# Splitting the first load of a DMA-bound rotation kernel into 16 and 112 partitions

## The chip, the cores and the metric

The kernel runs on one core of one Trainium2 chip. The metric is the device time of one execution in microseconds (us); lower is better. All runs are with a granted TensorE clock of 1.0 (TensorE does nothing here).

## The reference

```
x: float32 of shape (32, 3, 256, 256)
return np.rot90(x, k=-1, axes=(-2, -1)).astype(np.float32)
```

Each of 96 images of 256 x 256 is turned by 90 degrees. Nothing is computed: 25.17 MB are read from HBM, rearranged on the chip, and 25.17 MB are written back.

## The kernel before

The work is cut into 12 slabs of 2 MB. All loads are issued first, from the SyncE queue, then VectorE transposes slab after slab in place of the slab before, and each finished slab is stored by the same queue. Slab 0 is turned first into PSUM and stored last.

```python
P, RI, RO, I = 128, 16, 8, 2          # F = RO * W = 2048 elements, 8 KB
ld8_v  = rows_in.rearrange("(n i p r) w -> n p i (r w)", i=I, p=P, r=RO)
ld16_v = rows_in.rearrange("(n i m r) w -> n i m (r w)", i=I, m=Q * K, r=RI)   # Q * K = 64
# ... units[n]: one SBUF tile of [P, I, F] for each slab, all resident

for n in range(n_slabs):
    if n == last:
        nc.sync.dma_start(out=units[n], in_=ld8_v[n])            # 2 MB
        continue
    for i in range(I):
        if n == 0:
            nc.sync.dma_start(out=units[n][:, i], in_=ld8_v[n][:, i])   # 1 MB, 128 rows of 8 KB
        else:                                                    # 1 MB, 64 rows of 16 KB, every 2nd partition
            nc.sync.dma_start(out=units[n][i::I].rearrange("p i f -> p (i f)"), in_=ld16_v[n, i])

# ... for each slab: two VectorE transposes, then stores from SyncE; slab 0 last
```

## Time and profile before

| | before |
|---|---|
| time, median of 6 runs | 124.09 us (123.96 to 124.23) |
| span of the profiled run | 122.2 us |
| packets on the 16 DMA engines, share of the span | 97.8% |
| VectorE busy | 76% |
| first packet starts | 1.74 us |
| full rate from about | 2.75 us |
| last store lands | 121.18 us |

The DMA engines move a transfer in packets, here one for each row (in the trace of the kernel before 3456 of 8 KB and 1280 of 16 KB), and an engine's part of a transfer has landed when it reports to the semaphore (16 reports for each of that trace's 37 transfers). A stretch line gives start:end, length, busy time of VectorE, ScalarE and GpSimd, the granted clock, the share of the DMA engines' time filled by packets, and the bytes of packets in GB/s. A packet counts in full in the stretch in which it starts, so a short stretch can show more than the true rate, and a share above 1. "The stream is late by d at so many MB" below means: the same count of bytes had been moved d us later than in the kernel before. It is worked out from all packets in the two traces, with the bytes of a packet spread evenly over its time; two further executions of the unchanged start, the control and the kernel with the last load in two, come out 0.07 and 0.08 us late at 10 MB, so a difference of 0.1 us is about the least that counts.

### The profile page before, as it was taken

What the parts mean: (1) busy time and instruction counts of PE and PEld (TensorE: products, weight loads), DVE (VectorE), ACT (ScalarE), POOL (GpSimd) and SP (SyncE); (2) the same over time, 40 slices, a digit from 0 to 9 for tenths busy, and PEclk for the clock granted to TensorE, in tenths of its full rate; (3) what the DMA queues carried; (4) which work ended last, traced back from release to release, by engine and by line L of the source; (5) the groups of instructions that cost most, each with busy time, mean ns of one, the idle gap of its engine ahead of it and who ended that gap; (6) DMA issues with size and microseconds to landing.
All of it is one profiled execution on the core that took longest, in us unless ns stands there. A gap on an engine that the chain in (4) does not pass through costs nothing.

```text
span 122.2 us, 134 instructions
## 1 busy us (share of the span) xinstructions
DVE 93.3 (76%) x24; ACT 5.0 (4%) x3; POOL 0.2 (0%) x4
## 2 busy tenths in 40 slices
DVE  0299999999999999999999999999999940000000
ACT  0000000000000000000040000000000651000000
POOL 0000000000000000000000000000000000000000
DMA  3999999999999999999999999999999999999993
GB/s 88 429 432 434 440 440 429 429 429 429 429 429 429 429 429 424 434 424 408 370 414 428 426 429 429 429 429 429 429 429 429 424 429 429 429 429 426 429 429 166
DMA packets 5584, 50.33 MB, mean 412 GB/s; under 512 B 592, under 2 KB 720, under 8 KB 848
## 3 DMA queue, kind: packets, MB, share of 16 engines
q1 hardware_dynamic: 5584, 50.33, 97.8%
HBM read 25.17 MB, written 25.17 MB: 412 GB/s over the span
## 4 chain that ended last, share of the span: by engine, by line
DMA 57%; DVE 13%; issue 7%; DVEq 3%; ACT 2%; SPq 1%
DMA u<-in_x_dram 39%; DMA out_dram<-u 18%; DVE u L82 10%; DVE u L76 3%; DVEq L119 3%; ACT u L92 2%; SPq L66 1%; SPq L89 0%
## 5 line engine op out<-in xcount | busy, mean ns | idle before, releaser
L82 DVE STREAM_TRANSPOSE u<-u 128x2048 f32<-128x2048 f32 x20 | 78.0, 3948 | 0.3
L76 DVE STREAM_TRANSPOSE turned<-u 128x2048 f32<-128x2048 f32 x2 | 7.6, 3828 | 5.5 <-DMA u<-in_x_dram 5.5
L76 DVE STREAM_TRANSPOSE u<-u 128x2048 f32<-128x2048 f32 x2 | 7.8, 3953 | 0.0
L92 ACT COPY u<-turned 128x2048 f32<-128x2048 f32 x2 | 3.7, 1866 | 33.8 <-DVE u L76 33.8
L92 ACT ACT_TABLE_LOAD x1 | 1.3, 1283 | 62.4 <-DMA u<-in_x_dram 62.4
L108 POOL MEMSET const-bfloat16-1.0<- 128x1 bf16 x1 | 0.1, 102 | 0.0
L108 POOL MEMSET const-uint8-127<- 128x1 uint8 x1 | 0.1, 102 | 0.0
L108 POOL MEMSET const-float32-0.0<- 128x1 f32 x1 | 0.1, 99 | 0.2 <-issue 0.2
L108 POOL MEMSET const-float32-1.0<- 128x1 f32 x1 | 0.1, 99 | 0.0
## 6 DMA issues: line engine op xcount, KB each, us to landing
u<-in_x_dram SPq DMA_DIRECT2D x22, 1024.0 KB, 19.6
out_dram<-u SPq DMA_DIRECT2D x11, 2048.0 KB, 25.0
u<-in_x_dram SPq DMA_DIRECT2D x1, 2048.0 KB, 22.5
out_dram<-u SPq DMA_DIRECT2D x1, 1024.0 KB, 20.2
out_dram<-u SPq DMA_DIRECT2D x1, 896.0 KB, 20.2
out_dram<-u SPq DMA_DIRECT2D x1, 128.0 KB, 20.6
```

The costliest lines, as they stand in the source:

```text
L66: nc.sync.dma_start(out=units[n][:, i], in_=ld8_v[n][:, i])
L76: nc.vector.transpose(out=dst[:, :, ::-1, ::-1], in_=src)
L82: nc.vector.transpose(out=dst[:, cs], in_=src[:, cs])
L92: nc.scalar.copy(out=units[last][:, i], in_=turned0[:, i])
L108: nc = _bacc.Bacc("TRN2", target_bir_lowering=False, num_devices=1)
L119: with _tile.TileContext(nc) as tc:
```

## The change

In the trace of the kernel before, the first 1 MB transfer is 128 packets of 8 KB and reports 16 landings, so eight rows for each of the 16 DMA engines if they are dealt out evenly. They do not start together: eight first packets start from 1.738 to 1.826 us, eight more only from 2.405 to 2.530. The idea of the change is that a first transfer with a single row for each engine gets all 16 engines going at once.

```diff
+    FIRST = 16
...
             if n == 0:
-                nc.sync.dma_start(out=units[n][:, i], in_=ld8_v[n][:, i])
+                for a, b in ((0, FIRST), (FIRST, P)) if i == 0 else ((0, P),):
+                    nc.sync.dma_start(out=units[n][a:b, i], in_=ld8_v[n][a:b, i])
```

## The prediction

> **What bounds the kernel now.** I read the page first, for who is busy; then the pieces of the chain that ended last, for what sets the end; then a table of stretches, for the transfer rate in the middle and at the two ends; and last the records of single packets in the first three microseconds, because the change sits there. The page:
>
> ```profile
> span 122.2 us, 134 instructions
> DVE 93.3 (76%) x24; ACT 5.0 (4%) x3; POOL 0.2 (0%) x4
> ...
> DMA  3999999999999999999999999999999999999993
> GB/s 88 429 432 434 440 440 429 429 429 429 429 429 429 429 429 424 434 424 408 370 414 428 426 429 429 429 429 429 429 429 429 424 429 429 429 429 426 429 429 166
> ...
> q1 hardware_dynamic: 5584, 50.33, 97.8%
> ```
>
> See that the 16 DMA engines are full in every slice but the first and the last, near 429 GB/s, and that their packets fill 97.8% of the span, while VectorE has 24% to spare. The 25.17 MB in and 25.17 MB out are fixed by the problem. 50.33 MB at 429 GB/s is 117.3 us; the span is 122.2, so moving things about can win at most 4.9 us. The chain, in order of time (start, length, what):
>
> ```profile
> 0.67 0.06 issue
> 0.73 0.39 SPq L66
> 1.12 0.05 issue
> 1.17 0.42 SPq L66
> 1.59 0.05 issue
> 1.64 8.74 DMA u<-in_x_dram
> ...
> 99.26 1.87 ACT u L92
> ```
>
> See that one issue of the first slab takes 0.39 us and the next starts 0.44 us after it. The last scalar copy ends at 101.13 us, and its store lands 20 us later: it queues behind stores already issued, so neither VectorE nor the copy is on the path at the end. The stretches (start:end, length, engines' busy time, clock, share of the DMA engines, GB/s):
>
> ```profile
> 1.50:1.75 0.25, 0.00 (x0) 0.00 (x0) 0.00 (x0) 1.00 0.08 33
> 1.75:2.00 0.25, 0.00 (x0) 0.00 (x0) 0.00 (x0) 1.00 1.62 229
> 2.00:2.25 0.25, 0.00 (x0) 0.00 (x0) 0.00 (x0) 1.00 0.53 66
> 2.25:2.50 0.25, 0.00 (x0) 0.00 (x0) 0.00 (x0) 1.00 0.57 197
> 2.50:2.75 0.25, 0.00 (x0) 0.00 (x0) 0.00 (x0) 1.00 0.27 98
> 2.75:3.00 0.25, 0.00 (x0) 0.00 (x0) 0.00 (x0) 1.00 1.00 426
> ...
> 100.00:120.00 20.00, 0.00 (x0) 1.12 (x1) 0.00 (x0) 1.00 1.01 428
> 120.00:120.50 0.50, 0.00 (x0) 0.00 (x0) 0.00 (x0) 1.00 0.55 229
> 120.50:121.20 0.70, 0.00 (x0) 0.00 (x0) 0.00 (x0) 1.00 0.06 23
> ```
>
> See that the engines start at about 1.74 us but do not run at full rate before about 2.75; from then to the end the stream has no hole. In the packet records, eight first packets of 8 KB start between 1.738 and 1.826, and six of these take 0.89 to 1.15 us where a steady one takes 0.309. The other two take 0.32, and their successors stall for 1.05 us. A second group of eight starts only between 2.405 and 2.530. By about 2.8 us every engine has done one packet, give or take 0.2. So the time is: start of the stream, plus 50.33 MB at a fixed rate, plus a tail of 1.0 us after the last landing at 121.18. The time of 124.06 is 1.9 us over the span, which I carry along unchanged.
>
> [...] The trace of before shows 16 landings for every transfer, of 128 or 64 rows. [...] the second eight engines start 0.667 us after the first eight, which for the 64 rows of half a transfer is 10.4 ns a row. [...] Here the first packet comes 1.01 us after the issue begins and 0.62 after it ends, so no early start before the end of the issue is seen. [...] The trace before has no load confined to 16 partitions, [...] its 64-row loads use every second partition, [...] and run at full rate.
>
> **The change, part by part.** No byte, VectorE or ScalarE instruction changes. The order of instructions shows one more transfer on the SyncE queue, a first transpose that waits for two semaphores instead of one, and the eight rotating transfer semaphores shifted by one.
>
> - Issue: one more of about 0.39 + 0.05 = 0.44 us on the SyncE queue. Later loads are issued 0.44 us later. Each 1 MB of load takes 2.45 us to move and about 0.64 to issue, so this is hidden from the third transfer on. Cost on the path: 0, except for the second.
> - What it is meant to win: with one row for each engine, [...]. The most that a perfect start could win is read from the stretches: up to 3.00 us the bytes are 0.25 x (33 + 229 + 66 + 197 + 98 + 426) = 262 KB; at 428 GB/s from 1.74 they would be 539 KB. The difference, 277 KB, is 0.65 us.
> - What takes it back: the 16 packets are done after 0.31 us, at about 2.1 to 2.2. The 112-row transfer is issued at 1.17 instead of 0.73, so its first packets come at 1.17 + 1.01 = 2.18, and by the same 10.4 ns a row the second eight get theirs 56 x 10.4 = 0.58 us later, at 2.76. These engines have then done one packet, as they have by 2.8 before. With this sum the eight late engines win some 0.05 to 0.1 us, not 0.6, and the end is set by the slowest engine.
> - [...]
> - Later in the kernel: the shift of the semaphores keeps every store waiting on the same load as before, since both moved by one. VectorE starts about 0.1 to 0.4 us earlier or later; its slack at the end is 20 us. Cost 0.
>
> The sum is a small gain of about 0.1 [...], half believed, [...]: about 0.05 us off, 124.0.
>
> **The rivals.**
> - The start is won in full: all 16 engines move from 1.8 us on and the second transfer arrives in time. For it: two first packets of before took only 0.32 us, so data can flow that early. Against: their next packets stalled for 1.05. It would give 124.06 - 0.65 = 123.4.
> - A cold start that lasts until about 2.45 us whatever is asked for, visible as the stall of early and late engines alike up to about 2.75. Then nothing is won; for it speaks that early and late starters finish together. 124.06.
> - The second issue is the new wait: if the stall repeats for the second transfer, [...], engines idle for up to 0.44 us. 124.5.
> - [...]
>
> **Range and chances.** Every mechanism acts once, in the first 3 us, and is bounded by 0.65 us of gain [...]. Two per cent is 2.5 us, which none reaches. The runs of before differ by 0.27 us. I predict 124.0, with 123.5 to 124.6 holding it 8 times in 10, chances of 0.01 faster, 0.98 same and 0.01 slower.
>
> **What would show it.** In the changed kernel's stretches, rates between 1.75 and 2.25 well above 229 and 66 with a hole after them mean that the first packets went early and the second issue came late; a full rate from 1.8 on means the first rival; [...]. Everything from 10 us on should be the same profile, shifted by the same amount. I would be wrong if that shift differed between start and end, if the rate in the middle changed, or if the time left 123.4 to 125.2.

The sum came to 124.0, which is 124.06 less 0.05, half of the gain of 0.1. Against the gain stood a loss of about 0.3 us, weighed at less than half, and with it a rival at 125.2 (the upper end of the last range named): estimates, on grounds that no trace or run shows. The estimate: the second eight engines would start 8 x 10.4 ns = 0.08 us after the first instead of 0.67, the 10.4 ns a row being the 0.667 us in the trace of the kernel before over 64 rows. That 16 rows are one for each engine was assumed; the trace of the changed kernel shows 16 first packets between 1.754 and 1.928 us.

## The result, and the profile after

The changed kernel took 124.58 us (median of 6 runs, 124.45 to 124.70) against 124.09 before. The ratio is 1.0037, with a 95% interval of 1.0025 to 1.0050: a loss of 0.4%, small but clear of noise. A ratio here is the mean time of one kernel's runs over that of the other's of the same rounds, so it is not quite the ratio of the medians.

The page after:

```profile
span 122.8 us, 136 instructions
...
GB/s 80 304 448 427 432 427 432 432 432 427 427 427 427 427 427 427 427 427 387 424 418 425 427 427 427 430 427 427 430 427 430 430 427 430 427 427 427 430 430 205
...
u<-in_x_dram SPq DMA_DIRECT2D x1, 896.0 KB, 5.6
...
u<-in_x_dram SPq DMA_DIRECT2D x1, 128.0 KB, 3.1
```

The rate in the middle is the same. The second slice, 3.1 to 6.1 us, shows 304 GB/s where before had 429: the loss sits there. The stretches of the changed kernel:

```profile
1.75:2.00 0.25, 0.00 (x0) 0.00 (x0) 0.00 (x0) 1.00 2.33 524
2.00:2.25 0.25, 0.00 (x0) 0.00 (x0) 0.00 (x0) 1.00 0.00 0
2.25:2.50 0.25, 0.00 (x0) 0.00 (x0) 0.00 (x0) 1.00 0.43 66
2.50:2.75 0.25, 0.00 (x0) 0.00 (x0) 0.00 (x0) 1.00 0.56 131
2.75:3.00 0.25, 0.00 (x0) 0.00 (x0) 0.00 (x0) 1.00 0.56 131
...
4.00:5.00 1.00, 0.00 (x0) 0.00 (x0) 0.00 (x0) 1.00 1.02 328
5.00:6.00 1.00, 0.00 (x0) 0.00 (x0) 0.00 (x0) 1.00 1.10 320
...
60.00:62.00 2.00, 1.97 (x2) 0.00 (x0) 0.00 (x0) 1.00 1.00 418
```

And two of the same stretches in the kernel before:

```profile
4.00:5.00 1.00, 0.00 (x0) 0.00 (x0) 0.00 (x0) 1.00 1.01 426
...
60.00:62.00 2.00, 1.97 (x2) 0.00 (x0) 0.00 (x0) 1.00 0.93 334
```

Three things are to be seen.

1. The early start happens. All 16 first packets begin between 1.754 and 1.928 us. They take 0.57 to 0.60 us each, so the 0 GB/s from 2.00 to 2.25 is no idle time: by the packets' durations the engines are all busy there. The gap follows when the first packets end (2.33 to 2.52 us), as the second ones straggle in from 2.343 to 3.1: from 2.50 to 2.75 the engines are busy for 28% of the time, from 2.75 to 3.00 for 52%. Up to 10 us they idle for 0.40 us each, against 0.30 before, and by 3.0 us 176 KB have been moved, against 210 KB before and 186 KB in the control. So the start is neither won nor lost by much.
2. From 3 to 6.5 us the engines are full (share 1.01 to 1.10 in the whole stretches), yet only 311 to 328 GB/s move. A packet of 8 KB takes 0.43 us (median of those that start from 4 to 6 us) instead of 0.309. Each packet counted with its excess over 0.309, this comes to 0.94 us for each engine between 3.0 and 6.5 us. The stream is 1.23 us late at 12 MB.
3. At 60 to 62 us the roles change: before has a slow spell of 334 GB/s at the end of the load phase, after has none. Of the 1.24 us late at 24 MB, 0.87 remain at 27 MB. At the end the last engine finishes 0.69 us late (121.87 against 121.18), as the engines end closer together (within 0.29 instead of 0.62 us), and the span is 0.6 longer.

So the change costs 1.2 us where it acts, and more than half of that does not show in the time.

### The profile page after: what moved, and what is told of

The parts are those of the page before. It is cut to its first block, busy times and chain, and to the rows that moved or that the text cites. A ratio compares the mean times of both kernels' runs of the same rounds, so it can differ in the third digit from the quotient of the medians.

```text
span 122.8 us, 136 instructions
## 1 busy us (share of the span) xinstructions
DVE 93.3 (76%) x24; ACT 5.0 (4%) x3; POOL 0.2 (0%) x4
## 4 chain that ended last, share of the span: by engine, by line
DMA 52%; DVE 16%; issue 10%; DVEq 3%; ACT 2%; SPq 0%
DMA u<-in_x_dram 36%; DMA out_dram<-u 16%; DVE u L84 13%; DVE u L78 3%; DVEq L121 3%; ACT u L94 2%; SPq L68 0%; SPq L88 0%
```

## The experiments

Theory P: which partitions a transfer writes sets its rate. The rival, theory L: the second transfer is issued too late, and the engines run dry. A third question is what gives 0.37 us back near 60 us (the expectations say 0.35). Every kernel gave a correct result, and all but the control differ from the kernel before (or from the changed one) only by the lines shown. Ratios are to runs of the kernel before on the same chip in the same rounds, whose medians were 123.95 to 124.01.

### Halves: the same sizes on other partitions

```diff
 # halves_contiguous
-nc.sync.dma_start(out=units[n][:, i], in_=ld8_v[n][:, i])
+for rows in (slice(0, 64), slice(64, P)) if i == 0 else (slice(0, P),):
+    nc.sync.dma_start(out=units[n][rows, i], in_=ld8_v[n][rows, i])
 # halves_interleaved: (slice(0, P, 2), slice(1, P, 2))
```

> The first 1 MB load as two transfers of 64 neighbouring partitions (0 to 63, then 64 to 127). Theory P ([...] the changed kernel's loss comes from which partitions one transfer writes; [...]): [...] packets of the first megabyte run at about half rate, and the stream is 1.2 us (if the second half slips in beside the first) to 2.4 us late at 10 us; time 125 to 126.5. Theory L (late issue: the engines run dry because the second transfer is issued 0.44 us after the first): the first part gives each engine 4 packets, 1.24 us of work, so no hole; stream within 0.2 us of before, time 124.1.

> As the run with two contiguous halves, but even partitions first, then odd ones: the same count, sizes and engines (4 packets each), only the partitions differ. Theory P: [...] no slow packets after the start; stream 0 to 0.3 us earlier than before; time 123.8 to 124.1. Theory L: no hole either, 124.1. The difference between this run and the contiguous halves is P's: 1 us or more under P, none under L.

Measured: contiguous 125.70 us, ratio 1.0138 (1.0124 to 1.0153); interleaved 124.20 us, ratio 1.0030 (1.0007 to 1.0054). The stretches of the contiguous halves:

```profile
3.00:4.00 1.00, 0.00 (x0) 0.00 (x0) 0.00 (x0) 1.00 1.18 262
4.00:5.00 1.00, 0.00 (x0) 0.00 (x0) 0.00 (x0) 1.00 1.04 229
5.00:6.00 1.00, 0.00 (x0) 0.00 (x0) 0.00 (x0) 1.00 0.92 197
```

and of the interleaved halves:

```profile
3.00:4.00 1.00, 0.00 (x0) 0.00 (x0) 0.00 (x0) 1.00 1.01 426
4.00:5.00 1.00, 0.00 (x0) 0.00 (x0) 0.00 (x0) 1.00 1.05 442
5.00:6.00 1.00, 0.12 (x1) 0.00 (x0) 0.00 (x0) 1.00 0.98 377
```

The engines are full in both, but with 64 neighbouring partitions the rate is halved: a packet takes 0.61 us (median from 4 to 6 us) instead of 0.309. Count, size and engines are the same; only the choice of partitions differs, and the medians differ by 1.50 us. That is what theory P foresaw, and L foresaw none of it. One rival is left: other partitions here also mean other rows of x, so the reads from HBM change along with the writes, and no run moves one without the other. Against it speaks that the later loads read 1 MB in one piece into 64 partitions, but into every second one, and run at the full 428 to 430 GB/s (10 to 40 us, in both). Why neighbouring partitions are slow is not seen in the trace.

The stream of the interleaved halves is about 0.3 us late from its first megabyte on, which neither theory foresaw: the issue of a 64-row transfer took 0.54 us instead of 0.39, the first packet started at 2.04 instead of 1.74, and that is the 0.3. (The profiled run took 124.58 us, more than the median.)

### Columns: the same first bytes on all partitions

```diff
-nc.sync.dma_start(out=units[n][:, i], in_=ld8_v[n][:, i])
+for a, b in ((0, W), (W, F)) if i == 0 else ((0, F),):
+    nc.sync.dma_start(out=units[n][:, i, a:b], in_=ld8_v[n][:, i, a:b])
```

> The first 1 MB load as 1 KB of every one of 128 partitions (131 KB, the same bytes as the 16 rows) and then 7 KB of each. Theory L: the first part is again only about 0.37 us of work for an engine (8 packets of 46 ns), the second issue comes 0.44 us later, so the hole is there as with 16 and 112 rows; stream 0.3 to 1.2 us late. Theory P: [...] no packet of the second part is slower than the 272 ns that a 7 KB store packet takes, and the stream is within 0.3 us of before; time 123.8 to 124.3.

Measured: 124.05 us, ratio 1.0002 (0.9987 to 1.0017). The second part's packets of 7 KB took 0.272 us (median from 3 to 4 us), as foreseen, and the stream was 0.3 to 0.4 us late up to 24 MB. Most of that is L's part: up to 10 us the engines idled for 0.54 us each, against 0.30 before. A split whose first part is 131 KB, 8 KB for each of the 16 engines on average, with the second issue 0.44 us later, was harmless for the time here, where every partition is in both parts.

### The 112 rows first, the 16 after

```diff
+for rows in (slice(0, 112), slice(112, P)) if i == 0 else (slice(0, P),):
+    nc.sync.dma_start(out=units[n][rows, i], in_=ld8_v[n][rows, i])
```

> 112 partitions first and the last 16 after them: the 112-row shape without an early start and without a first transfer that is used up before the second is issued. Theory P: [...] packets of 0.37 to 0.45 us instead of 0.31 again, and the stream is 0.8 to 1.3 us late at 10 us, time 124.4 to 125.4. Theory L: engines have 7 packets, no hole, time 124.1.

Measured: 125.68 us, ratio 1.0136 (1.0121 to 1.0151), the stream 1.93 us late at 10 MB: more than P expected. Its stretches:

```profile
4.00:5.00 1.00, 0.00 (x0) 0.00 (x0) 0.00 (x0) 1.00 1.04 287
5.00:6.00 1.00, 0.00 (x0) 0.00 (x0) 0.00 (x0) 1.00 1.23 205
```

Here the first transfer has 112 packets, seven for each of the 16 engines if they are dealt out evenly, so a late second issue cannot be the cause. L falls for this kernel. The packets that start from 3.0 to 5.2 us, nearly all of them of the 112 rows, have a median of 0.46 us and an excess of 0.70 us for each engine. Those from 5.2 to 7.5, when the engines pass to the 16 rows and to the transfer after them, take up to 1.05 us and add 1.13. So 16 rows that come behind another transfer seem to cost more than 16 rows that come first; no run tests that alone.

### Sixteen rows first, without the 112

```diff
+nc.sync.dma_start(out=units[last][:16, 0], in_=ld8_v[0][:16, 0])   # overwritten by the last load
 for n in range(n_slabs):    # as before: 128 rows in one transfer
```

> The kernel before with 16 rows (partitions 0 to 15, 131 KB, as in the change) loaded first into the tile of the last slab, which is overwritten later, and then the whole 1 MB load of 128 rows as before: the early start, [...] and the second issue of the change, without the 112-row transfer. It moves 131 KB more, 0.31 us. If the 112-row shape makes the slow packets, packets after 3.5 us are 0.31 us again and the stream at 10 us is 0.2 to 0.5 late; time 124.2 to 124.5. If the 16 rows [...] block what follows, packets stay slow to about 6 us as in the changed kernel and the stream is 1.2 us or more late; time 124.9 or more.

Measured: 124.43 us, ratio 1.0039 (1.0014 to 1.0063), with 131 KB (0.31 us) more to move. Its stretches:

```profile
4.00:5.00 1.00, 0.00 (x0) 0.00 (x0) 0.00 (x0) 1.00 0.95 401
5.00:6.00 1.00, 0.00 (x0) 0.00 (x0) 0.00 (x0) 1.00 1.01 418
```

The packets from 3 us on have a median of 0.309 us again. For the same count of bytes, the extra ones included, the stream is late by 0.23 to 0.28 us up to 24 MB, most of it idle time (0.51 us for each engine up to 10 us, against 0.30 before). In the time the kernel loses 0.48 us (124.43 - 123.95), of which 0.31 are the extra bytes. So a first transfer of 16 rows costs some 0.17 us, its early start included; the interval of the ratio allows for -0.1 to 0.5, so no cost at all is possible. It does not slow the packets that follow; it is the 112-row transfer whose packets are slow.

### Both parts issued at once, from two queues

```diff
-nc.sync.dma_start(out=units[n][a:b, i], in_=ld8_v[n][a:b, i])
+queue = nc.scalar if a else nc.sync
+queue.dma_start(out=units[n][a:b, i], in_=ld8_v[n][a:b, i])
```

> The changed kernel with the 112-row transfer issued by ScalarE at the same moment as SyncE issues the 16 rows, so that nothing waits for a second issue; the transfers themselves are unchanged. Theory L (late issue): the hole between 2.3 and 2.8 us closes and the time falls to 124.1 or below. Theory P [...]: the hole closes, but packets between 3 and 6 us are still 0.37 to 0.45 us and the stream stays 0.8 us or more late at 10 us; time 124.3 to 124.7.

Measured: 124.49 us, ratio 1.0049 (1.0028 to 1.0070). Its stretches:

```profile
2.25:2.50 0.25, 0.00 (x0) 0.00 (x0) 0.00 (x0) 1.00 0.00 0
2.50:2.75 0.25, 0.00 (x0) 0.00 (x0) 0.00 (x0) 1.00 1.98 459
...
4.00:5.00 1.00, 0.00 (x0) 0.00 (x0) 0.00 (x0) 1.00 1.09 328
5.00:6.00 1.00, 0.00 (x0) 0.00 (x0) 0.00 (x0) 1.00 0.96 270
```

The gap closed, as both theories expected. That no packet starts from 2.25 to 2.50 is again no idle time, since the first packets last until 2.26 to 2.80 us; from 2.75 on the engines are full, and up to 10 us they idle for 0.15 us each instead of 0.40. Yet the stream is 1.12 us late at 10 MB instead of 1.23. So some 0.1 us of the lateness went with the second issue, which is little more than two executions differ by, and the slow packets (median 0.44 us from 4 to 6 us) stayed. P holds; L explains at most a small part.

### Two attempts at a better split

```diff
 # sixteen_spread_first
+for rows in (slice(0, P, 8), slice(4, P, 8), slice(2, P, 4), slice(1, P, 2)) if i == 0 else (slice(0, P),):
+    nc.sync.dma_start(out=units[n][rows, i], in_=ld8_v[n][rows, i])
 # thirty_two_spread_first: (slice(0, P, 4), slice(2, P, 4), slice(1, P, 2))
```

> The first 1 MB load in four transfers of 16, 16, 32 and 64 rows, each spread over the partitions with a step (every 8th from 0, every 8th from 4, every 4th from 2, every odd one): again one packet for each engine first[...]. Theory P: the early start keeps its worth and the loss is gone: no packet of the first megabyte after 3 us over 0.35 us; the stream at 2 MB is within 0.3 us of before or up to 0.4 earlier; time 123.6 to 124.2. If what hurts is the use of 16-row transfers or the number of issues (four, 0.44 to 0.6 us each), the stream is 0.6 us or more late and the time over 124.4.

> As the run with 16 spread rows first, but 32 (every 4th from 0), 32 (every 4th from 2) and 64 (odd ones): [...]two packets an engine, one issue fewer. Theory P: no slow packets after the start; the stream within 0.3 us of before; time 123.7 to 124.2. The 64-row loads took 0.6 us to issue and their first packet came 0.3 us later than with 128 or 16 rows; if 32 rows are slow to issue too, the stream is 0.2 to 0.4 us late and the time 124.2 to 124.4.

Measured: 125.15 us, ratio 1.0105 (1.0088 to 1.0122), and 126.02 us, ratio 1.0168 (1.0152 to 1.0184). Both miss what P expected, no slow packets after the start since each part is spread over the partitions; in the first it is the other case named there, 16-row transfers or the number of issues, whose numbers came. The stretches of the second:

```profile
4.00:5.00 1.00, 0.00 (x0) 0.00 (x0) 0.00 (x0) 1.00 0.60 180
5.00:6.00 1.00, 0.00 (x0) 0.00 (x0) 0.00 (x0) 1.00 0.88 295
```

Part of it is issuing: these transfers took 0.54 to 0.60 us to issue, and a first packet started only at 2.07 to 2.12 us. Up to 10 us the engines idled for 0.95 and 1.24 us each, against 0.30 before. The rest is slow packets of up to 1.1 us (1.4 in the second) until about 9 us, although each part is spread over the partitions. In the second kernel the engines' landings of one transfer drift apart to 2.45 us. So theory P in the form "a transfer that is spread over the partitions runs at full rate" is too simple. Why these packets are slow was not shown: the packet records name no engine. That stays open.

### The control, and what gives time back near 60 us

```diff
 # same_as_before: no edit
 # delayed_start, ahead of all loads:
+for j in range(3):
+    nc.sync.dma_start(out=tiny[:, j], in_=ld8_v[0][:16, 0, 16 * j : 16 * j + 16])
 # last_load_in_two (on before) and change_and_last_in_two (on the changed kernel):
-nc.sync.dma_start(out=units[n], in_=ld8_v[n])
+for i in range(I):
+    nc.sync.dma_start(out=units[n][:, i], in_=ld8_v[n][:, i])
```

> The kernel before, unchanged, as a control. In its profile the 2 MB load that ends the load phase has a slow spell at 59.3 to 60.9 us (packets of up to 775 ns), worth some 0.35 us, which the changed kernel and both others that were over 1 us late do not have, while the two variants that were 0.3 us late have it. If the spell belongs to the kernel and its timing, it is there again within 1 us of 59.3; if it is a chance event of one execution, it is gone or elsewhere. Time 124.0, ratio 1.000 within 0.002.

> The kernel before with three tiny loads of 16 rows of 64 bytes into a scratch tile ahead of its first load: the stream starts some 1.3 us later (3 issues of 0.44), with every later transfer, its partitions and sizes unchanged. It asks whether the 0.35 us given back at the end of the load phase come from the stream being late. If lateness alone takes the slow spell away, the stream is about 1.3 late at 20 MB and 0.9 to 1.0 late after 26 MB, time 124.9 to 125.1. If the spell belongs to the order of transfers as before, it is still there, shifted by 1.3 us to about 60.6, and the time is 125.3.

> The kernel before with only its last load (2 MB, both halves of 128 rows in one transfer) issued as two of 1 MB. It asks whether the slow spell near 60 us belongs to the form of that one transfer. If it does, no packet between 58 and 62 us is over 0.33 us, the stream gains 0.35 us there, and the time is 123.6 to 123.8. If the spell comes from what surrounds it, it is still there and the time stays at 124.0.

> The changed kernel with its last load also in two transfers. If the changed kernel wins back 0.35 us only because the slow spell of that load is absent from it, this edit gives it nothing: time 124.5 to 124.6, while the same edit takes before down to some 123.7, so that the two differ by 0.8 to 0.9. If the edit helps both alike, the give-back comes from elsewhere.

Measured: the control took 123.90 us, ratio 1.0002 (0.9989 to 1.0015), and its slow spell was there again:

```profile
60.00:62.00 2.00, 1.97 (x2) 0.00 (x0) 0.00 (x0) 1.00 0.90 316
```

It belongs to the kernel, not to one execution. The delayed start took 125.13 us, ratio 1.0099 (1.0083 to 1.0114); its stream was 1.46 us late at 22 MB and 1.26 at 27 MB, so lateness by itself gave back 0.20 us, about half of the 0.37. The last load in two took 123.95 us, ratio 0.9998 (0.9977 to 1.0019): the long packets went, but not the loss, as the stretch shows:

```profile
60.00:62.00 2.00, 1.97 (x2) 0.81 (x1) 0.00 (x0) 1.00 0.85 334
```

The engines stand idle for some 12% of that stretch (by the packets' durations) instead of moving slow packets, at the same 334 GB/s. The same edit on the changed kernel gave 124.53 us, ratio 1.0044 (1.0024 to 1.0064), no difference to the changed kernel either. It also repeats that kernel's start: its stream was 1.26 us late at 10 MB. So the spell is real and repeats, the changed kernel escapes it, and its cause is not the form of that load alone, nor the lateness of the stream alone. The five other kernels with slow packets in the first megabyte gave back 0.33 to 0.40 us between 24 and 26 MB, the columns 0.15, the kernel with 16 extra rows 0.12 and the interleaved halves 0.02. Why they differ stays open.

No variant beat the kernel before, so there is no better version to show.

## Why the prediction was right or wrong

- **The bound.** Right: the time is the stream of transfers, nothing else moved it, and the tail after the last landing was the foreseen 1.0 us. VectorE's first transpose began 1.4 us later (6.87 against 5.50) and cost nothing.
- **The early start.** Right in kind: the second group of eight engines no longer waits, and 16 rows came out within 0.174 us, 10.9 ns a row beside the 10.4 foreseen. The step that followed was off: the second transfer's packets were put at 2.18 and 2.76 us and came from 2.34 to 3.1. So the gain of 0.05 to 0.1 us was not there. The rival of a cold start that lasts whatever is asked for fits the start best: as much had been moved by 3.0 us as in the control (176 and 186 KB).
- **The second issue as the new wait.** It was named as a rival with up to 0.44 us. The sign that the prediction gave for it, high rates up to 2.25 with a hole after them, came true (524, then 0 GB/s), and would have misled: at the 0 GB/s the engines were busy, the true gap after it cost 0.1 us of idle time more than before, and issuing both at once won back some 0.1 us of the stream and nothing clear in the time.
- **The partitions.** This is the term that was mis-sized, and it sets the sign. The prediction took a loss of about 0.3 us for it and weighed it at less than half; that was the author's estimate, on grounds that were not shown. The runs show 0.94 us of extra packet time for each engine, most of the 1.23 us by which the stream was late: near the loss in the rival at 125.2. The part for the 16 rows is small: as an extra load they cost 0.17 us beyond their own bytes, though the interval includes 0. The term that failed is that of the 112 rows: their packets took a median of 0.43 us instead of 0.309 behind the 16 rows, and 0.46 us as the first transfer. A transfer to 64 neighbouring partitions ran at about half of the rate, 197 to 262 GB/s where the kernel before shows 401 to 442 (3 to 7 us in both). Why was not shown.
- **The rest of the kernel.** Wrong: everything after 10 us was to be the same profile shifted by the same amount. The shift fell from 1.24 to 0.87 us near 60 us and to 0.69 at the last landing. Without that, the time would have been about 125.1 (124.58 + 1.24 - 0.69).
- **The sum.** 124.0 was predicted and 124.58 measured, just inside 123.5 to 124.6, with the change of 0.05 us in the wrong direction. Nor does 124.0 follow from the sum's own weights: half of a gain of 0.1 is 0.05, and the loss of 0.3 outweighs that as soon as it is given more than one chance in six. The class, within 2%, followed from the bound that every mechanism acts once in the first microseconds, and for the loss that held; the nearness of the number is partly luck: it owes some 0.5 us to a give-back that was not foreseen.

## What to carry to other kernels

Split a transfer along the free dimension, or by every second partition, rather than into blocks of neighbouring partitions: the first cost nothing here and the second 0.3%, and of two splits with the same sizes and counts the one into blocks took 1.50 us more. Finer stepped splits, in three or four parts, lost 1.05 and 1.68%, so test before you trust a step. Engines that are all busy did not mean the full rate here: with 112 rows the share was 1.01 to 1.10 from 3 to 6 us, at 311 to 328 GB/s instead of 426 to 442. So look at the time of single packets, not at the engines' busy share. And when a stream is late at the start, follow the lateness to the end before crediting the change with the final difference.

## What else the traces show

- The landings of the 16 rows come late. Each of their 16 packets took 0.57 to 0.60 us in the changed kernel, and 0.41 to 0.43 in the kernel with 16 extra rows. In the changed kernel they land from 3.46 to 3.83 us, 1.1 to 1.3 us after the packets' ends, against 0.36 for the first transfer of the kernel before.
- The issue of each of the first loads took 0.38 to 0.43 us when the first transfers had 16, 112 or 128 neighbouring rows of 8 KB or less, and 0.54 to 0.60 us in the four kernels that began with 64 neighbouring rows or with stepped rows, where the 128-row transfer after them took that long too. The first packet then came 0.3 us later.
- A slow spell at the end of the load phase repeats (334 GB/s from 60 to 62 us, 316 in the control), and some small changes at the start remove it, for a reason that stays open.
